# A two-layer hybrid decoder: new tokens in one stationary tile, 1/rms through memory, spatial weights loaded earlier, new tokens' scores behind the attention

## The chip, the cores and the metric

One core of a Trainium2 chip. The metric is the device time of one execution in microseconds (us); smaller is better. The kernel before takes 2384.72 us (median of three runs, 2384.2 to 2386.24).

## The reference

Two layers work on 1024 prompt positions and on 8 new tokens (one for each of 8 requests), which share the weights. All numbers are fp32. Of each layer this matters here:

```python
h = rms_norm(x, norm_g)
(a_b, a_c, a_h, a_gate, s_q, s_k, s_v, s_gate,
 c_u, c_v, c_gate, d_q, d_k, d_v, d_gate) = split(h @ w_in)
...
vn  = layer_norm(c_v, v_ln_g, v_ln_b)
y_c = c_u * (tril(w_spatial) @ vn + b_spatial)
...
for g, (win, dil) in enumerate(((128, 1), (512, 4), (2048, 16))):
    o, lse = attention(dq[g], dk[g], dv[g])
alpha = softmax(lses, axis=0)
y_d = concat(o[g] * alpha[g])
merged = sum(sigmoid(h @ w_merge) * ((branch * silu(gate)) @ w_branch))
x = x + merged @ w_out
```

Branch A is a short convolution, B a sliding-window attention, C the mix over chunks of 128 positions with the matrices w_spatial (six of 128x128), D an attention over three pairs of heads ("groups" 0 to 2) with growing stride, whose three results are weighted by alpha. The new tokens attend to cached keys and values.

## The kernel before

**Products.** x, normalised but for the factor 1/rms, lies with channels on the partitions: eight tiles hh[k] of the rounded (hi) part and eight tiles hl[k] of the rest, 1032 columns each, the first 8 of them the new tokens. Every weight tile is split in the same way (`split_w`: ACT makes wh, POOL makes wl). A product takes three matmuls per 128 channels: hi x hi, lo x hi and hi x lo. Most go through `fm_tile` and `mm_cols` (lines 178 to 182), weights stationary, 344 columns moving. The results go through three accumulators of PSUM ("acc").

**Values.** Where rows must lie on the partitions, `tm_group` (line 341) makes the tokens stationary and moves the weights: eight blocks of 128 tokens and a ninth (n = 8) of the 8 new ones, 24 matmuls each (lines 372, 375, 376). It is called three times in a layer: by `tm_v` for 256 columns (S_V and the first of D_V), then for C_V (384 columns), then by `tm_v` for the other 256 of D_V. In the ninth block the stationary operand has 8 columns.

**1/rms.** The factor 1/rms of a token is multiplied in later. rtok holds it with tokens on the partitions (line 326); rr holds it as a row of 1032 columns, the same on all partitions, and the rotary tables cosT and sinT are multiplied by it. From rtok to rr the kernel makes a diagonal matrix per block (dg, line 332, DVE), multiplies it by ones (line 333, PE), copies the result (line 336, ACT) and multiplies cosT (line 337, DVE) and sinT (line 338, POOL), in three pieces of the row.

**Spatial mix.** Behind the third of these groups lngb (biases and LN factors), and wsp (w_spatial) are loaded; line 465 transposes wsp on PE (six 128x128, "ms" in PSUM).

**New tokens in D and B.** `Decode.scores` (line 647): line 656 transposes the tokens' query, DVE copies it (qr), SP stores it (qscr, line 659) and loads it again on all partitions (qb, line 661); POOL multiplies by the cached keys (line 662), DVE sums up (sd, line 663). `decode_finish` transposes sd (line 680), takes the softmax on DVE and ACT (lines 681 to 709), transposes the weights back (line 713) and gives `values`, six parts of 2 + 16 small matmuls (lines 731 and 733). For the prompt, `attend_d` stores max and denominator of its softmax (sscr, line 872 in group 2); al loads them (line 920), alpha is made on DVE, transposed (line 934), stored (ascr, line 938) and broadcast in six loads (at, line 944). Then y of branch C is loaded from memory (yscr, 516 KB each), split into yh and yl (line 979), and multiplied with w_branch in turn with h @ w_merge.

**Order.** Each engine works its list off in order; a scheduler writes the lists. SP's list holds nearly all loads; `load` (line 90) ties a load to the `dist`-th last mark, a mark being the first matmul of a tile or of every fourth block. A load also waits until its buffer is free and until earlier transfers with the same completion counter have landed. "dec" is a ring of three tiles for v, the cached keys and values, qb, y, lngb, wsp; "ct" one of four.

## Time and profile before

| | |
|---|---|
| median of 3 runs | 2384.72 us |
| profiled execution | 2387.34 us, span 2385.6 us |
| mean granted clock of TensorE | 0.991 |
| PE busy | 2365.5 us (99%) |
| DVE, ACT, POOL busy | 38%, 29%, 35% |
| DMA | 113 GB/s over the span |

The span is what the profile covers, from its first to its last instruction; the time of the execution has a little around it. PE is TensorE, and SP issues transfers. "Granted clock" is the share of 2.4 GHz that the chip let TensorE have. A matmul's time in a timeline reaches beyond the start of the next one, so the cost of one in a stream is the distance of two starts. Rows of the timeline that follow one another and are alike stand in one row with their count (x).

### The profile page before, as it was taken

Reading aid. Unit: us, or ns where it says so; the run is one execution under the profiler, and the core shown is the slowest. Engines: PE = TensorE matmul, PEld = TensorE weight load, DVE = VectorE, ACT = ScalarE, POOL = GpSimd, SP = SyncE. Lnnn points to the kernel's source line nnn. Section 1 sums busy time; section 2 is a strip of 40 time slices with the busy share of each in tenths; the row PEclk is TensorE's granted clock in tenths of the full one; section 3 lists DMA queues with packets and bytes.
Section 4 is the critical chain, followed back from the end, with each engine's and each line's share of the span. In section 5 each row is a group of like instructions: output and inputs, shape, how many; then the busy total and the mean of one; then the engine's idle time right before and its main releaser. Section 6 shows DMA issues by size and latency. Waiting matters only on the chain.

```text
span 2385.6 us, 38754 instructions
## 1 busy us (share of the span) xinstructions
PE 2365.5 (99%) x15896; PEld 2305.1 (97%) x15896; DVE 895.2 (38%) x1938; ACT 687.4 (29%) x1522; POOL 843.5 (35%) x556
## 2 busy tenths in 40 slices
PE   7999999999999999999999999999999999999999
PEld 6999999999999999999999999999999999999999
DVE  4345466335312222324333455554452221213143
ACT  5133432223212222223322244323231221212243
POOL 3333234432223444434442322353322233444330
PEclk9999999999899999999999999999989999999999
DMA  7342423433322212224542423244442122222232
GB/s 237 98 123 79 119 69 109 132 102 106 100 71 88 77 55 97 64 70 123 150 146 72 145 72 98 69 151 113 111 126 67 58 91 66 98 67 62 75 99 101
DMA packets 295962, 235.82 MB, mean 99 GB/s; under 512 B 52756, under 2 KB 279696, under 8 KB 293416
## 3 DMA queue, kind: packets, MB, share of 16 engines
q1 hardware_dynamic: 267952, 206.25, 28.8%
q10 hardware_dynamic: 27832, 27.10, 4.1%
q8 instruction: 124, 2.03, 0.4%
q14 instruction: 54, 0.44, 0.1%
HBM read 192.35 MB, written 76.47 MB: 113 GB/s over the span
## 4 chain that ended last, share of the span: by engine, by line
PE 98%; DVE 1%; DMA 0%; ACT 0%; SPq 0%; issue 0%; ACTq 0%; DVEq 0%
PE acc L181 27%; PE acc L182 27%; PE acc L178 27%; PE acc L372 2%; PE acc L375 2%; PE acc L376 2%; PE sc L540 2%; PE ms L569 2%; PE ms L558 1%; PE ms L733 1%; PE ms L479 0%; PE ms L1042 0%; DMA wr<-in_w_in_dram 0%; DVE xT L264 0%; DVE h0l L209 0%; PE ms L333 0%
## 5 line engine op out<-in xcount | busy, mean ns | idle before, releaser
L156 POOL TENSOR_TENSOR wl<-wr,wh 128x384 fp32r<-128x384 f32 (+2 forms) x228 | 476.9, 2093 | 827.3 <-ACT wh L154 698.7
L181 PE MATMUL acc<-h1l,wh 128*128 128x344 f32 x1584 | 511.5, 323 | 0.0
L182 PE MATMUL acc<-h0h,wl 128*128 128x344 f32 x1584 | 510.4, 323 | 0.0
L178 PE MATMUL acc<-h0h,wh 128*128 128x344 f32 x1584 | 509.3, 322 | 0.9 <-DVE xT L264 0.9
L178 PE MATMUL acc<-h1h,wh 128*128 128x344 f32 x1584 | 510.2, 322 | 0.0
L182 PE MATMUL acc<-h1h,wl 128*128 128x344 f32 x1584 | 509.5, 322 | 0.0
L181 PE MATMUL acc<-h0l,wh 128*128 128x344 f32 x1584 | 508.9, 321 | 0.0
L154 ACT ACTIVATE wh<-wr 128x384 fp32r<-128x384 f32 (+2 forms) x228 | 205.2, 901 | 421.4 <-PE acc L181 393.6
L1005 DVE TENSOR_TENSOR th<-acc,rr 128x344 f32<-128x344 f32 x192 | 99.1, 516 | 553.5 <-PE acc L182 553.5
L181 PEld LDWEIGHTS acc<-h1l,wh 128*128 128x128 f32 x1584 | 299.9, 189 | 4.2 <-issue 3.6
L181 PEld LDWEIGHTS acc<-h0l,wh 128*128 128x128 f32 x1584 | 299.2, 189 | 3.9 <-issue 3.5
L182 PEld LDWEIGHTS acc<-h1h,wl 128*128 128x128 f32 x1584 | 299.7, 189 | 2.8 <-issue 2.3
L178 PEld LDWEIGHTS acc<-h0h,wh 128*128 128x128 f32 x1584 | 299.1, 189 | 2.8 <-issue 1.2
L182 PEld LDWEIGHTS acc<-h0h,wl 128*128 128x128 f32 x1584 | 298.6, 189 | 2.9 <-issue 2.3
L178 PEld LDWEIGHTS acc<-h1h,wh 128*128 128x128 f32 x1584 | 299.6, 189 | 1.4 <-issue 1.0
L1011 POOL TENSOR_TENSOR mg<-mg,th 128x344 f32<-128x344 f32 x144 | 134.0, 931 | 303.3 <-DVE th L1010 303.3
L1006 ACT ACTIVATE th<-th 128x344 f32<-128x344 f32 x192 | 94.3, 491 | 496.9 <-DVE th L1005 496.4
L178 PE MATMUL acc<-yh,wh 128*128 128x344 f32 x576 | 184.4, 321 | 0.0
L182 PE MATMUL acc<-yh,wl 128*128 128x344 f32 x576 | 184.3, 320 | 0.0
L181 PE MATMUL acc<-yl,wh 128*128 128x344 f32 x576 | 184.1, 320 | 0.0
L181 PE MATMUL acc<-ml,wh 128*128 128x344 f32 (+3 forms) x384 | 123.2, 321 | 0.0
L182 PE MATMUL acc<-mh,wl 128*128 128x344 f32 (+3 forms) x384 | 123.0, 321 | 0.0
(278 smaller groups left out, 3256.6 us busy)
## 6 DMA issues: line engine op xcount, KB each, us to landing
wr<-in_w_merge_dram SPq DMA_DIRECT2D x64, 512.0 KB
out_dram<-in_cache_dil_kv_dram SPq DMA_DIRECT2D x128, 255.9 KB
wr<-in_w_in_dram SPq DMA_DIRECT2D x60, 512.0 KB
y<-yscr SPq DMA_DIRECT2D x18, 516.0 KB
wr<-in_w_branch_dram SPq DMA_DIRECT2D x48, 192.0 KB
wr<-in_w_in_dram SPq DMA_DIRECT2D x32, 256.0 KB
wr<-in_w_out_dram SPq DMA_DIRECT2D x16, 512.0 KB
out_dram<-in_cache_dil_kv_dram SPq DMA_DIRECT2D x16, 511.0 KB
```

What stands on the lines that cost most here:

```text
L154: act.activation(hi, raw, AF.Copy)
L156: pool.tensor_tensor(lo, raw, hi.bitcast(F32), op=ALU.subtract)
L178: mm = pe.matmul(ps[:, :n], hi[:, k], xh[k][:, cs], start=(k == 0), stop=False)
L181: pe.matmul(ps[:, :n], hi[:, k], xl[k][:, cs], start=False, stop=False)
L182: pe.matmul(ps[:, :n], lo[:, k], xh[k][:, cs], start=False, stop=(k == kt - 1))
L372: mm = pe.matmul(ps[:M, :N], lh, hi[:, k % kk], start=(k == 0), stop=False)
L375: pe.matmul(ps[:M, :N], ll, hi[:, k % kk], start=False, stop=False)
L376: pe.matmul(ps[:M, :N], lh, lo[:, k % kk], start=False, stop=(k == KT - 1))
L540: pin(pe.matmul(ps[:, h, a * 256:a * 256 + u.nk], u.qs[h], u.ks[h], start=True, stop=True))
L1005: dve.tensor_tensor(t, pg[:, :CH], rr[:, cs], op=ALU.mult)
L1006: act.activation(t, t, AF.Tanh, scale=0.5)
L1011: pool.tensor_tensor(mg[m][:, cs], mg[m][:, cs], t, op=ALU.add)
```

## The change

Four things. (1) The hi and lo columns of the new tokens are copied once per layer into one tile hd of 40 columns (hi in 0 to 7, lo in 32 to 39, zeros between); the ninth block is 16 matmuls in place of 24, and ACT and DVE add the two halves. (2) rtok is stored in a row of memory (rscr, in pieces of 4 bytes) by ACT, and SP loads it on all partitions as rr; cosT and sinT are multiplied once. (3) lngb and wsp are loaded before the second query tile, right behind the call of the first group of values. (4) In D the new tokens' scores are called after the attention of their group.

```diff
--- before.py
+++ after.py
@@ -65,7 +65,7 @@
         return psM.tile([P, 512], F32, tag="ms", name="ms")
 
     def ctmp(name):
-        return tp.tile([P, CH], F32, tag="ct", name=name, bufs=4)
+        return tp.tile([P, MIX], F32, tag="ct", name=name, bufs=4)[:, :CH]
 
     def dscr(name, shape):
         return dr.tile(shape, F32, tag=name, name=name)
@@ -324,18 +324,13 @@
         for ps_, M in ((slice(0, 8), P), (slice(8, 9), NS)):
             act.activation(rtok[:M, ps_], pt_[:M, ps_], AF.Sqrt, bias=epst[:M], scale=1.0 / DM)
             dve.reciprocal(rtok[:M, ps_], rtok[:M, ps_])
-        for n0, n1 in ((8, 9), (0, 4), (4, 8)):
-            ps = pmisc()
-            M = NS if n0 == 8 else P
-            for n in range(n0, n1):
-                dg = sm.tile([P, P], F32, tag="dg", name="dg", bufs=2)
-                dve.tensor_scalar(dg[:M, :M], ident[:M, :M], rtok[:M, n:n + 1], None, op0=ALU.mult)
-                pe.matmul(ps[:, (n - n0) * P:(n - n0) * P + M], onesm[:M], dg[:M, :M], start=True, stop=True)
-            cs = slice(0, NS) if n0 == 8 else slice(NS + n0 * P, NS + n1 * P)
-            w = cs.stop - cs.start
-            act.activation(rr[:, cs], ps[:, :w], AF.Copy)
-            dve.tensor_tensor(cosT[:, cs], cosT[:, cs], rr[:, cs], op=ALU.mult)
-            pool.tensor_tensor(sinT[:, cs], sinT[:, cs], rr[:, cs], op=ALU.mult)
+
+        rscr = dscr(f"rscr{l}", [T])
+        act.dma_start(rscr[0:NS], rtok[:NS, 8])
+        act.dma_start(rscr[NS:T].rearrange("(n i) -> i n", i=P), rtok[:, 0:8])
+        sp.dma_start(rr, rscr.partition_broadcast(P))
+        dve.tensor_tensor(cosT, cosT, rr, op=ALU.mult)
+        pool.tensor_tensor(sinT, sinT, rr, op=ALU.mult)
         cw = sm.tile([P, 3, 3], F32, tag="cw", name="cw")
         for t in range(3):
             load(cw[:, :, t], i["conv_w"][l, t].rearrange("(j p) -> p j", p=P), 2)
@@ -366,6 +361,15 @@
                 cols = blkcols(n) if n < 8 else slice(0, NS)
                 M = P if n < 8 else NS
                 ps = pacc()
+                if n == 8:
+                    for k in range(KT):
+                        for a, w in enumerate(ws[k // kk]):
+                            pe.matmul(ps[:40, :N], hd[:, k], w[:, k % kk], start=(k + a == 0), stop=(k + a == KT))
+                    s = tp.tile([NS, MIX], F32, tag="ct", name="sd", bufs=4)[:, :N]
+                    act.activation(s, ps[32:32 + NS, :N], AF.Copy)
+                    dve.tensor_tensor(s, s, ps[:NS, :N], op=ALU.add)
+                    consumer(n, M, s)
+                    break
                 for k in range(KT):
                     hi, lo = ws[k // kk]
                     lh, ll = hh[k][:, cols], hl[k][:, cols]
@@ -375,6 +379,12 @@
                     pe.matmul(ps[:M, :N], ll, hi[:, k % kk], start=False, stop=False)
                     pe.matmul(ps[:M, :N], lh, lo[:, k % kk], start=False, stop=(k == KT - 1))
                 consumer(n, M, ps[:M, :N])
+
+        hd = sm.tile([P, KT, 40], F32R, tag="hd", name="hd")
+        pool.memset(hd.bitcast(F32), 0.0)
+        for k in range(KT):
+            for a, h in enumerate((hh, hl)):
+                pool.tensor_copy(hd[:, k, 32 * a:32 * a + NS], h[k][:, 0:NS])
 
         vcs = slot("vcs")
         vsam, cvs = vcs[:NS, 0:512], vcs[:NS, 512:512 + MIX]
@@ -406,6 +416,15 @@
 
         kB, qB = rope(kq[0]), [rope(kq[1])]
         tm_v([(S_V, P), (D_V, P)], 0)
+        lngb, wsps = dec([P, T], "lngb"), dec([P, T], "wsp")
+        wsp = wsps[:, 0:6 * P].rearrange("p (g s) -> p g s", g=6)
+        bsps = [lngb[:, 6 * P:7 * P], lngb[:, 7 * P:8 * P], wsps[:, 6 * P:7 * P]]
+        for h in range(2):
+            for j in range(3):
+                load(bsps[j][h * 64:(h + 1) * 64], bview[h, j].partition_broadcast(64), 2)
+        load(lngb[:, 0:MIX], i["v_ln_g"][l].partition_broadcast(P), 2)
+        load(lngb[:, MIX:2 * MIX], i["v_ln_b"][l].partition_broadcast(P), 2)
+        load(wsp, i["w_spatial"][l].rearrange("g t s -> t g s"), 2)
         qB.append(rope_tile(w_pair(l, S_Q, 1), "qB1"))
         cvt = [sl.tile([P, 2, MIX], F32, tag="slot", name=f"cv{q}") for q in range(4)]
         lnst = sm.tile([P, 9, 6], F32, tag="lnst", name="lnst")
@@ -438,14 +457,6 @@
             return t
 
 
-        lngb, wsps = dec([P, T], "lngb"), dec([P, T], "wsp")
-        wsp = wsps[:, 0:6 * P].rearrange("p (g s) -> p g s", g=6)
-        bsps = [lngb[:, 6 * P:7 * P], lngb[:, 7 * P:8 * P], wsps[:, 6 * P:7 * P]]
-        for h in range(2):
-            for j in range(3):
-                load(bsps[j][h * 64:(h + 1) * 64], bview[h, j].partition_broadcast(64), 2)
-        load(lngb[:, 0:MIX], i["v_ln_g"][l].partition_broadcast(P), 2)
-        load(lngb[:, MIX:2 * MIX], i["v_ln_b"][l].partition_broadcast(P), 2)
         for n in range(9):
             M = P if n < 8 else NS
             if n == 0:
@@ -457,7 +468,6 @@
             dve.tensor_tensor(v, v, lngb[:M, 0:MIX], op=ALU.mult)
             dve.tensor_tensor(v, v, lngb[:M, MIX:2 * MIX], op=ALU.add)
         store_later(2, o["chunk_v_s"][l].rearrange("b s c -> (b s) c"), cvs)
-        load(wsp, i["w_spatial"][l].rearrange("g t s -> t g s"), 2)
         wsT = dec([P, 6, P], "wsT")
         for g0 in (0, 3):
             ps = pmisc()
@@ -887,8 +897,8 @@
         decD = Decode("D")
         rows, attention = branch_d(0, ends)
         conv_a(0, rows)
+        attention()
         decD.scores(0, dqs[0], dks[0])
-        attention()
         conv_a(1)
         in_a(0)
         decB = Decode("B")
@@ -903,15 +913,15 @@
         rows, attention = branch_d(1)
         in_a(1)
         rows()
+        attention()
         decD.scores(1, dqs[1], dks[1])
-        attention()
         out_a(1)
         conv_a(2)
         rows, attention = branch_d(2)
         sg0 = gate_d(0)
         rows()
+        attention()
         decD.scores(2, dqs[2], dks[2])
-        attention()
         in_a(2)
         values_d = decD.finish(OD)
 
```

The scheduler orders the lists anew. In the rows here line numbers of the changed kernel are up to 10 higher.

**PE, first group of values, layer 0** (acc and ms are PSUM tiles, h0h and h0l the parts of h, dg the diagonal matrix). Before:

```order
229 L372 MATMUL acc<-wh,h0h_132 128x256
230 L375 MATMUL acc<-wh,h0l_140 128x256
231 L333 MATMUL ms<-dg,onesm 128x8
232 L333 MATMUL ms<-dg,onesm 128x128
233 L376 MATMUL acc<-wl,h0h_132 128x256
```

Changed; the group begins at row 217:

```order
287 L379 MATMUL acc<-wh,h0l_143 128x256
288 L380 MATMUL acc<-wl,h0h_135 128x256
289 L475 MATMUL ms<-ident,wsp 128x128 x6
290 L376 MATMUL acc<-wh,h0h_128 128x256
291 L379 MATMUL acc<-wh,h0l_136 128x256
```

Line 333 is gone from the group, and the six transposes of wsp, which stood behind the third group, come after 72 of its matmuls. It is so in both layers.

**SP, at the same place, layer 0.** Before (the loads of lngb and wsp stood in rows 37 to 43, behind the second weights of the third group):

```order
26 L93 DMA cosT<-const_cos_dram 128x1032
27 L93 DMA sinT<-const_sin_dram 128x1032
28 L93 DMA wr<-in_w_in_dram 128x2x384 x3
29 L93 DMA out_dram<-in_cache_swa_kv_dram 4x2x16256
30 L93 DMA wr<-in_w_in_dram 128x2x384
```

Changed:

```order
28 L93 DMA wr<-in_w_in_dram 128x2x384
29 L93 DMA lngb<-in_b_spatial_dram 64x128 x2
30 L93 DMA wsp<-in_b_spatial_dram 64x128
31 L93 DMA lngb<-in_b_spatial_dram 64x128
32 L331 DMA rr<-rscr_526 128x1032
33 L93 DMA lngb<-in_b_spatial_dram 64x128
34 L93 DMA wsp<-in_b_spatial_dram 64x128
35 L93 DMA lngb<-in_v_ln_g_dram 128x384
36 L93 DMA lngb<-in_v_ln_b_dram 128x384
37 L93 DMA wsp<-in_w_spatial_dram 128x6x128
38 L93 DMA wr<-in_w_in_dram 128x2x384 x2
```

rr's load and all of lngb and wsp stand ahead of three of the four weight loads of C_V; rr waits for the two stores of rscr, and the load of v_ln_b (row 36) for the counter that rr's landing raises. In layer 1 rr stands right ahead of v_ln_b, which doesn't wait for it.

**PE, branch D of layer 0, end of group 2's attention** (line 569, 579 in the changed kernel). Before:

```order
3237 L182 MATMUL acc<-h0h_132,wl 128x344
3238 L569 MATMUL ms<-pt,v_5477 64x128 x4
3239 L680 MATMUL ms<-ident,sd 8x128 x6
3240 L178 MATMUL acc<-h0h_133,wh 128x344
3241 L181 MATMUL acc<-h0l_141,wh 128x344
```

Changed, at the same place:

```order
3199 L579 MATMUL ms<-pt,v_5432 64x128 x4
3200 L666 MATMUL ms<-ident,dqs_5304 8x128
3201 L690 MATMUL ms<-ident,sd 8x128 x2
3202 L181 MATMUL acc<-h0l_139,wh 128x344
3203 L182 MATMUL acc<-h0h_131,wl 128x344
```

Changed, at the first matmul with yh (pn and pd are the transposed weights, vcs and cD the new and cached values):

```order
3326 L743 MATMUL ms<-pd,cD_5727 64x1 x8
3327 L741 MATMUL ms<-pn,vcs 64x8
3328 L743 MATMUL ms<-pd,cD_5727 64x1 x8
3329 L178 MATMUL acc<-yh_6133,wh 128x344
3330 L178 MATMUL acc<-h0h_128,wh 128x344
```

Line 656, ahead of the attention before, is now behind it (row 3200), and the transposes of sd come in three pairs: 21 wide matmuls lie between the first and the second, 50 between the second and the third, and 39 between the third and line 723 (713 before). Before, 73 lay between line 680 and line 713, 20 more ahead of the values and 12 between them and the first matmul with yh; now the six parts follow line 723 in one piece and the first matmul with yh follows at once.

## Rows read from the trace of the kernel before

**Rows 1.** The page: span, and busy time of each engine (share, instructions).
```profile
span 2385.6 us, 38754 instructions
...
PE 2365.5 (99%) x15896; PEld 2305.1 (97%) x15896; DVE 895.2 (38%) x1938; ACT 687.4 (29%) x1522; POOL 843.5 (35%) x556
```

**Rows 2.** Waits of PE, whole span: in total, times, longest (us).
```profile
PE ms L333 <- DVE dg L332: 3.8, 3, 1.5
```

**Rows 3.** PE timeline, layer 0: start us, us, engine line op operands xcount [idle before].
```profile
50.42 0.28 PE L372 MATMUL acc<-wh,h0h 128*128 128x256 f32 x1
...
51.60 0.28 PE L375 MATMUL acc<-wh,h0l 128*128 128x256 f32 x1
...
79.92 0.28 PE L372 MATMUL acc<-wh,h0h 128*8 128x256 f32 x1
...
82.67 0.32 PE L178 MATMUL acc<-h0h,wh 128*128 128x344 f32 x1
...
127.55 0.34 PE L372 MATMUL acc<-wh,h0h 128*8 128x384 f32 x1
...
131.80 0.38 PE L540 MATMUL sc<-kB,qB 64*128 64x128 f32 x2
```

**Rows 4.** PE timeline, layer 1: first group of values, first and next matmul.
```profile
1222.38 0.38 PE L372 MATMUL acc<-wh,h1h 128*128 128x256 f32 x1
...
1251.61 0.32 PE L178 MATMUL acc<-h1h,wh 128*128 128x344 f32 x1
```

**Rows 5.** Stretches: PE, PEld, DVE, ACT, POOL busy (count), PEclk, DMA share, GB/s.
```profile
56.80:60.20 3.40, 3.40 (x19) 3.40 (x18) 0.29 (x1) 0.00 (x0) 0.00 (x0) 0.50 0.97 241
599.50:613.20 13.70, 13.70 (x91) 13.57 (x90) 7.00 (x9) 3.38 (x4) 2.52 (x2) 0.50 0.95 245
1770.30:1784.00 13.70, 13.70 (x91) 13.54 (x92) 6.85 (x9) 3.11 (x4) 3.80 (x2) 0.50 0.95 247
```

**Rows 6.** DVE timeline: end of 1/rms, both layers.
```profile
51.51 0.15 DVE L326 RECIPROCAL rtok<-rtok 8x1 f32<-8x1 f32 x1 [1.27 <-ACT rtok L325]
...
1222.79 0.29 DVE L326 RECIPROCAL rtok<-rtok 128x8 f32<-128x8 f32 x2 [21.97 <-ACT rtok L325]
```

**Rows 7.** ACT queue, SP queue, DVE: sscr in 16-byte pieces, then al.
```profile
571.81 0.63 ACTq L872 DMA_DIRECT2D sscr<-std  x1
...
577.31 0.37 SPq L920 DMA_DIRECT2D al<-sscr  x1
...
580.43 0.17 DVE L924 TENSOR_TENSOR mx<-al 128x16 f32<-128x16 f32 x1 [2.38 <-DMA al<-sscr]
```

**Rows 8.** SP queue, POOL, DVE: the new tokens' query rows in branch D.
```profile
342.62 0.30 SPq L659 DMA_DIRECT2D qscrD<-qr  x1
...
343.90 0.35 SPq L661 DMA_DIRECT2D qb<-qscrD  x1
...
347.92 2.40 POOL L662 TENSOR_TENSOR qb<-qb,cD 128x1024 f32<-128x1024 f32 x1 [0.84 <-DMA qb<-qscrD]
...
350.35 1.22 DVE L663 TENSOR_REDUCE sd<-qb 128x16 f32<-128x1024 f32 x1 [0.48 <-POOL qb L662]
```

**Rows 9.** SP queue: the six broadcasts of the prompt's group weights.
```profile
595.17 4.04 SPq L944 DMA_DIRECT2D at<-ascr  x6
```

**Rows 10.** DVE and ACT: softmax of the new tokens, then the first yh.
```profile
582.47 1.01 DVE L681 TENSOR_SCALAR sx<-ms 8x384 f32<-8x384 f32 x2
...
589.27 0.95 DVE L709 TENSOR_TENSOR sx<-sx,dw 8x774 f32<-8x774 f32 x1
...
606.91 1.06 ACT L979 ACTIVATE yh<-y 128x1032 fp32r<-128x1032 f32 x1 [10.53 <-DMA y<-yscr]
```

**Rows 11.** PE timeline, layer 0: end of D's attention, transposed weights, first yh.
```profile
579.79 0.66 PE L569 MATMUL ms<-pt,v 128*64 128x128 f32 x8
...
592.64 0.53 PE L713 MATMUL ms<-ident,sx 8*128 8x8 f32 x6
...
610.92 0.49 PE L178 MATMUL acc<-yh,wh 128*128 128x344 f32 x1
```

## The prediction

> **What bounds the kernel now.** I read the page's busy line first. TensorE (PE) is busy for 2365.5 us of a span of 2385.6, while VectorE (DVE), ScalarE (ACT) and GpSimd (POOL) stay under 40% [rows 1]. So an instruction taken from another engine gains nothing by itself, and time comes from three things only: fewer PE instructions, PE waits, and PE's clock. The list of PE's waits comes next: away from the start of the program its only large entry is the 1/rms matmul of line 333, 3.8 us in three waits [rows 2]. Then I read PE's timeline where the change touches it, and the granted clock by stretch. The clock falls to half (1.2 of 2.4 GHz) at 56.8 us for 3.4 us, and at the end of branch D of each layer for 13.7 us [rows 5]. The profiled execution took 2387.34 us, 2.6 above the median of 2384.72; the terms below come from its trace and are added to the median. About 0.2% (4.8 us) is what a measurement can tell from no change.
>
> **New tokens in one stationary tile.** In the group of 256 columns the prompt's matmuls start ten apart in 51.60-50.42 us, so one costs 0.118 us. The 24 with 8 stationary columns run from 79.92 to 82.67, so one costs 0.115; with 384 columns they run from 127.55 to 131.80, 0.177 each [rows 3]. The change makes 16 out of 24: eight less, in two groups at 0.115 and one at 0.177, in two layers: 2 x 8 x (0.115+0.115+0.177) = **6.5 us less**. The new ones have 40 stationary columns. That 8 and 128 columns cost the same to 0.003 us [rows 3] is why I charge nothing for the width.
> The Trainium skill, "TensorE: Matmul & The Clock Gate", section "LDWEIGHTS (loading the stationary operand)", says that the load grows with the number of columns, columns/1.2 ns. By that an estimate is 27 ns more for 40 columns than for 8, and if the load set the pace the 96 new matmuls would give back 2.6 of the 6.5 us; the rows at 8 and at 128 columns contradict that, so the sum leaves it out.
> The 16 copies per layer that fill the tile lie on POOL and are wanted only by the ninth block of a group; POOL is 35% busy [rows 1]. If that cover went, PE would wait there for a copy or two. The addition of the two halves per group, and the cosine and sine multiplied once instead of in three pieces, lie on ACT, DVE and POOL with the same cover; all of this I cost at nothing.
>
> **1/rms through memory.** Line 333 and what it did to the first group of values go. In layer 0 the group lasts from 50.42 to 82.67, 32.25 us [rows 3]. Its own matmuls are worth 192 x 0.118 + 24 x 0.115 = 25.4, so 6.8 us were lost to line 333, its waits and the half clock at 56.8. In layer 1 it lasts from 1222.38 to 1251.61 [rows 4], 29.2, so 3.8 were lost. Together **10.6 us less**, if nothing takes their place.
>
> **Spatial weights one group ahead.** Something does. PE now meets the six transposes of the spatial weights after only 72 matmuls of that group, 72 x 0.118 = 8.5 us after its start: 58.9 us in layer 0, 1230.9 in layer 1. Those weights stand on SP's queue behind the broadcast of 1/rms (rr), which has to wait for the store of 1/rms, and in layer 0 the load before them (v_ln_b) waits in turn for rr's landing.
> Layer 0: 1/rms is there at 51.66 [rows 6]. The store has 4-byte pieces. Bounds: 5.5 us, from the issue of sscr (1024 pieces of 16 bytes) at 571.81 to al's, which waits for it, at 577.31 [rows 7]; and 1.3 us, qscr's eight rows of 512 bytes, 342.62 to 343.90 [rows 8]. I take 5.5, since its pieces are nearest in size. rr is a broadcast of 516 KB; its neighbour qb (512 KB) takes 4.0 us, 343.90 to 347.92 [rows 8]. That makes 51.7+5.5+4.0 = 61.2, and with two issues of 0.37 [rows 7] 61.9. The spatial weights (393 KB) need between al's 3.1 us [rows 7] and qb's 4.0: they land at 65.0 to 65.9, and PE waits for 6 to 7 us. With the short store it would be 2 to 3. I take 6.0, and 1.7 for a stretch at half clock behind it, like that of 3.4 us at 56.8 [rows 5]: 7.7.
> ACT, whose stores and rotary copies share completion counters, is late too and so the evictions of these blocks are, but three accumulators hold exactly those 72 matmuls, so PE meets that delay at the same place and under the same wait.
> Layer 1: 1/rms at 1223.1 [rows 6], store 5.5, three issues of 0.37: the weights start at about 1229.5 beside rr, and land 3.1 us later if undisturbed, 8 if they share with all of rr: 1232.6 to 1237.5, a wait of 1.7 to 6.6; none with the short store. I take 3.5, and 0.9 for the clock: 4.4. Together **12.1 us more** (bounds 2 and 19).
>
> **Scores behind the attention.** For the first group of D and for the second the new tokens' chain has hundreds of matmuls before its result is read, and I cost it at nothing. For the third it is read at once. Between the last attention matmuls of D and the first with yh there are 105 wide matmuls now and 110 then, so the attention ends 0.8 us earlier, at 579.0 instead of 579.8 [rows 11]. The query's transpose now comes behind it, and on DVE its copy behind the prompt's softmax, which waits for al and ends at about 582. From there: store to broadcast 1.3, broadcast 4.0, POOL 2.4, DVE 1.2 [rows 8]: the scores are there at about 591.5, up to 592.7 with a slower broadcast. PE gets there after 71 matmuls of 344 columns, each 344/256 x 0.118 = 0.158, and 1 us of transposes, at about 591.3. The softmax then takes 582.47 to 590.22, 7.75 us [rows 10], while only 39 matmuls (6.2 us) are left beside it, so the transposes of the weights (line 713) run at about 600.0 instead of 592.64 [rows 11]. What hangs on them keeps its distance: behind line 713 stand the transposed group weights, their store, six broadcasts of 4.0 us of issue [rows 9], and only then y's first load on SP. Before, yh began 606.91-592.64 = 14.3 us after line 713 and took 1.06 [rows 10, 11]. So the first matmul with yh can run at 600.0+15.3 = 615.3, against 610.92 before [rows 11]: 4.4 us more. Before, 20 and 12 matmuls and the values filled that stretch; now the values alone do, and then PE stands. Half clock lasted 2.3 us beyond 610.92 [rows 5], a loss of 1.1; I expect 1 us more of it. So 5.4 per layer; layer 1 has the same half-clock stretch [rows 5], and I take the same. **10.8 us more** (bounds 3 and 16).
>
> **Sum:** -6.5-10.6+12.1+10.8 = +5.8, so **2390.5 us**.
>
> **The rivals.** (1) *The D end costs nothing.* Place: the first matmul with yh. If y lands within 10 us of line 713 instead of 14.3, because the values no longer hold its buffers, PE finds it there and the 10.8 fall away: 2384.72-6.5-10.6+12.1 = 2379.7, faster. For it: the buffers of the cached values come free sooner, since the six parts run in one piece. Against it: y's first load was issued as soon as the six broadcasts were (595.17+4.04) [rows 9], so the buffer didn't hold it. It decides from a landing at 610 on.
> (2) *The store is quick.* At qscr's 1.3 us [rows 8] the wait for the spatial weights shrinks to 2 us in layer 0 and nothing in layer 1: 2384.72-17.1+2+10.8 = 2380.4.
> (3) *The store is slow.* If 4-byte pieces take twice what 16-byte pieces took, 11 us, each layer waits 5.5 us longer: 2401.5. For it: 1024 pieces of 16 bytes took 5.5 us and eight of 512 bytes 1.3 [rows 7, 8], so pieces and not bytes set the price. Against it: the count of pieces is the same as sscr's.
> The Trainium skill, "DMA: Bandwidth & Descriptors", section "Specifications", says that a transfer under 512 bytes is read, changed and written back, which speaks against this part of the change; the two stores of the trace agree, and whether 4 bytes are dearer than 16 no row shows.
>
> **How the numbers follow.** Forecast 0.50, its own range 2384 to 2397: two thirds of it lie above 2389.5. Rival 1: 0.20, 2374 to 2385, 0.12 of it faster. Rival 2: 0.13, half of it faster. Rival 3: 0.12, slower. Rivals 1 and 2 together (about 2370): 0.05, faster. Faster is 0.12+0.06+0.05 = 0.23; slower 0.33+0.12 = 0.45; the same 0.32. The range takes the lower ends of rivals 1 and 2 and the high bounds of the forecast, 2384.72-17.1+17+16 = 2400.6, and leaves out the joint case and most of rival 3: 2376 to 2400.5.
>
> **What would show it.** In the profile after: six fewer busy us in the groups' last blocks; no line 333; PE's list of waits with the spatial transposes (line 475 there), longest about 6 us at 59 us, waiting for w_spatial; a second wait, of 5 us or so, at the first matmul with yh in each layer; a small one at line 723; and half clock behind each. It is wrong if line 475 waits for less than 3 us, if the first matmul with yh comes less than 12 us behind line 723, or if blocks with 40 columns start 0.14 us apart or more.

## The result and the profile after

The changed kernel takes 2419.12 us (median of four, 2417.68 to 2419.52), the kernel before 2384.46 on the same chip (2381.6 to 2386.24): 1.0145 times as long, 95% interval 1.0128 to 1.0163, or about 34.7 us more. The direction was predicted, the size was not: 2390.5 was forecast and 2400.5 was the upper end. The profiled execution took 2419.22 us, its span is 2417.5, and the mean granted clock 0.985 instead of 0.991. The two spans differ by 31.9 us and not by 34.7, since the profiled execution of the kernel before (2387.34) was 2.9 above its median here.

The page of the changed kernel, to set beside [rows 1]:

```profile
span 2417.5 us, 38609 instructions
...
PE 2362.2 (98%) x15812; PEld 2304.4 (95%) x15812; DVE 890.3 (37%) x1922; ACT 692.6 (29%) x1526; POOL 862.2 (36%) x586
```

PE is busy for 3.3 us less in a span that is 31.9 us longer, so the whole loss is waiting, and matmuls at half clock. The list of PE's waits of the changed kernel (in total, times, longest, us), of the entries that the change made:

```profile
PE ms L475 <- DMA wsp<-in_w_spatial_dram: 21.4, 2, 10.8
PE ms L723 <- DVE sx L719: 9.3, 2, 5.0
PE acc L178 <- ACT yh L989: 5.0, 2, 3.1
```

The mechanism of each was foretold: line 475 waits for w_spatial, line 723 and the first yh wait at the end of D, and line 333 is gone [rows 2]. But line 475 waits 10.8 and 10.6 us where about 6 and 3.5 were expected, line 723 waits 5.0 where "a small one" was, and the first yh waits 1.9 and 3.1 where 5 were. Starts on PE in the two traces show where the time is lost:

| PE starts (us) | before | after | later by |
|---|---|---|---|
| first group of values, layer 0 | 50.42 | 52.83 | 2.4 |
| behind that group | 82.67 | 91.28 | 8.6 |
| scores of B, behind C_V | 131.80 | 139.06 | 7.3 |
| first matmul with yh, layer 0 | 610.92 | 626.26 | 15.3 |
| first group of values, layer 1 | 1222.38 | 1238.92 | 16.5 |
| behind that group | 1251.61 | 1276.68 | 25.1 |
| first matmul with yh, layer 1 | 1782.17 | 1813.20 | 31.0 |
| end of the span | 2385.6 | 2417.5 | 31.9 |

The first groups lose 6.2 and 8.5 us, where +12.1 and -10.6 together had made +1.5 of both; between B's scores and layer 1 some 9 us go, and about 7 in layer 1.

The granted clock by stretch of the changed kernel answers to [rows 5] (columns as there):

```profile
29.40:32.80 3.40, 3.40 (x14) 3.40 (x13) 3.40 (x4) 2.90 (x7) 2.91 (x3) 0.50 0.87 335
63.50:77.20 13.70, 4.84 (x23) 4.87 (x24) 10.74 (x7) 1.21 (x3) 8.24 (x4) 0.50 0.96 240
609.70:630.10 20.40, 17.58 (x128) 17.04 (x129) 8.07 (x13) 3.21 (x4) 2.49 (x1) 0.50 0.69 170
1251.40:1261.60 10.20, 3.31 (x14) 2.94 (x15) 3.49 (x4) 1.21 (x3) 4.64 (x2) 0.50 0.96 273
1797.50:1818.00 20.50, 17.43 (x126) 17.13 (x126) 9.18 (x11) 3.19 (x3) 3.45 (x2) 0.50 0.69 169
```

In the two stretches of the first groups (63.5 and 1251.4) PE is busy for only 4.84 and 3.31 us, the rest is the wait itself; half clock thus cost about half of these, 2.4 and 1.7 us. At the end of D PE works 17.5 us at half clock instead of 13.7 [rows 5], 1.9 us more in each layer.

The chain of the first group in layer 0, from the timeline of all engines in the changed kernel (ACTq and SPq are the queues in which ACT and SP issue DMAs; to evict an accumulator is to copy its result out of PSUM, here line 401, so that it can be used again):

```profile
51.49 0.39 ACTq L330 DMA_DIRECT2D rscr<-rtok  x1
52.91 0.53 ACTq L329 DMA_DIRECT2D rscr<-rtok  x1
53.67 0.61 ACTq L290 DMA_DIRECT2D qs<-kB  x1
60.38 1.90 ACTq L290 DMA_DIRECT2D qs<-kB  x3
60.50 0.34 SPq L331 DMA_DIRECT2D rr<-rscr  x1
62.37 5.55 ACTq L290 DMA_DIRECT2D qs<-qB  x4
...
65.22 2.36 POOL L333 TENSOR_TENSOR sinT<-sinT,rr 128x1032 f32<-128x1032 f32 x1 [8.78 <-DMA rr<-rscr]
65.25 3.42 DVE L332 TENSOR_TENSOR cosT<-cosT,rr 128x1032 f32<-128x1032 f32 x1 [12.37 <-DMA rr<-rscr]
66.03 0.38 SPq L93 DMA_DIRECT2D wsp<-in_w_spatial_dram  x1
67.97 1.21 ACT L401 ACTIVATE vn<-acc,rtok 128x256 f32<-128x256 f32 x3 [13.21 <-DMA qs<-qB]
72.36 1.51 PE L475 MATMUL ms<-ident,wsp 128*128 128x128 f32 x6 [10.83 <-DMA wsp<-in_w_spatial_dram]
```

SP's side is the predicted chain with longer links: the store runs from 51.49 to about 60.4 (8.9 us, 5.5 were charged), rr takes 4.7, w_spatial 6.3 (66.03 to 72.36; 3.1 to 4.0 were charged) in a stretch where the DMA engines are 96% busy (the window from 63.5). But ACT's side is late too: its second load of a rotary copy (qs) issues at 60.38, when the store lands (it waits for the completion counter that the store raises), the eighth is issued at 67.9, and only then does ACT evict the first three blocks (67.97). In layer 1 the two sides end together; there the store was issued at 1240.10, and the second load of qs at 1247.66. The third row below holds the seventh and eighth load, which are part of the row above it:

```profile
1241.11 8.36 ACTq L290 DMA_DIRECT2D qs<-kB  x4
1249.56 9.67 ACTq L290 DMA_DIRECT2D qs<-qB  x4
...
1258.07 1.16 ACTq L290 DMA_DIRECT2D qs<-qB  x2
...
1259.28 1.21 ACT L401 ACTIVATE vn<-acc,rtok 128x256 f32<-128x256 f32 x3 [19.31 <-PE ms L475]
```

The transposes began at 1258.18 there, the evictions at 1259.28. The row names line 475 as what released the evictions, but ACT's queue was issuing qs until 1259.23. That the two end together is no accident: the seventh load waits for a completion counter which in this trace w_spatial's load raises, so it is issued when w_spatial lands, and in layer 1 ACT's lateness hangs on SP's.

### The profile page after: what moved, and what is told of

Read it like the earlier page. It is cut to its first block, busy times and chain, and to the rows that moved or that the text cites. A ratio compares the mean times of both kernels' runs of the same rounds, so it can differ in the third digit from the quotient of the medians.

```text
span 2417.5 us, 38609 instructions
## 1 busy us (share of the span) xinstructions
PE 2362.2 (98%) x15812; PEld 2304.4 (95%) x15812; DVE 890.3 (37%) x1922; ACT 692.6 (29%) x1526; POOL 862.2 (36%) x586
## 4 chain that ended last, share of the span: by engine, by line
PE 91%; DMA 4%; DVE 2%; ACT 1%; SPq 1%; issue 1%; POOL 0%; ACTq 0%; POOLq 0%; DVEq 0%
PE acc L178 26%; PE acc L182 26%; PE acc L181 26%; PE acc L376 2%; PE acc L380 2%; PE acc L379 2%; PE sc L550 2%; PE ms L579 2%; PE ms L568 1%; DMA wr<-in_w_in_dram 1%; DMA rscr<-rtok 1%; DMA y<-yscr 1%; DMA wsp<-in_w_spatial_dram 1%; DVE h0l L209 1%; PE ms L489 0%
## 5 line engine op out<-in xcount | busy, mean ns | idle before, releaser
L156 POOL TENSOR_TENSOR wl<-wr,wh 128x384 fp32r<-128x384 f32 (+2 forms) x228 | 486.1, 2134 | 800.4 <-ACT wh L154 747.2
```

Of the source, the lines that this page charges most:

```text
L156: pool.tensor_tensor(lo, raw, hi.bitcast(F32), op=ALU.subtract)
```

## Experiments

The expectations speak of two theories of the first group: A, SP's chain to w_spatial alone costs it; B, ACT's queue does, by the qs loads behind the store of 1/rms. D1 and D2 are two of the end of D: D1, the query's row is made too late; D2, the softmax is longer than the matmuls beside it. "The mark" is the first matmul of the ninth block, which the kernel before reports to `load` and the changed one doesn't. Ratios are to the kernel before on the same chip. The runs lie on several chips, on which the kernel before had medians from 2384.5 to 2386.7, so a difference of 2 us between runs of different chips says nothing.

### One part undone

**e1: lngb and w_spatial loaded where they were before.**

```diff
         tm_v([(S_V, P), (D_V, P)], 0)
-        lngb, wsps = dec([P, T], "lngb"), dec([P, T], "wsp")
...
-        load(wsp, i["w_spatial"][l].rearrange("g t s -> t g s"), 2)
         qB.append(rope_tile(w_pair(l, S_Q, 1), "qB1"))
```

> The changed kernel with part 3 undone: lngb and wsp are loaded where they were before, behind the third group of values. Theory A (the loss in the first group of values of each layer is PE waiting for w_spatial at line 475, 10.8 and 10.6 us, and the half clock behind each, 13.7 and 10.2 us long): both go, no wait of PE over 1 us stays in the group, the group falls to about 26 us in each layer, and the time to 2419 - 21.4 - 12 = about 2386 to 2394. Theory B (the 4-byte store of 1/rms holds up ACT's queue, whose loads of qs share its completion counters, so the evictions of the first blocks come late, and line 475 is only the place where PE stood when it happened): PE waits at the fourth block instead, for ACT's eviction, 4 to 6 us in each layer with half clock behind it, and the time is 2400 to 2412.

2420.82 us, 1.0147 (1.0132 to 1.0162): nothing gained, and slower than either theory said. PE's waits:

```profile
PE acc L376 <- ACT vn L401: 15.4, 2, 8.0
PE ms L723 <- DVE sx L719: 9.1, 2, 5.0
PE ms L475 <- DMA wsp<-in_w_spatial_dram: 5.4, 2, 3.3
```

With w_spatial out of the way PE stands at the next block for want of an evicted accumulator, for 15.4 us instead of 21.4, and waits 5.4 us more for w_spatial in the third group (the lost mark, see e7): 20.8 us in all. ACT's first eviction in that group comes at 67.57, behind the last qs issue. A alone falls, and B's wait is there, with 7.4 and 8.0 us instead of 4 to 6. ACT's queue is late by itself, and one wait had hidden the other.

**e2: 1/rms by matmul again** (lines 327 to 333 of the changed kernel replaced by lines 327 to 338 of the kernel before).

```diff
-        act.dma_start(rscr[0:NS], rtok[:NS, 8])
-        act.dma_start(rscr[NS:T].rearrange("(n i) -> i n", i=P), rtok[:, 0:8])
-        sp.dma_start(rr, rscr.partition_broadcast(P))
...
+                pe.matmul(ps[:, (n - n0) * P:(n - n0) * P + M], onesm[:M], dg[:M, :M], start=True, stop=True)
```

> The changed kernel with part 2 undone: rr is again made by nine diagonal matrices and matmuls, nothing of 1/rms goes through memory. The transposes of w_spatial still stand after 72 matmuls of the first group. Theory A: w_spatial no longer stands behind rr's load on SP and starts some 10 us earlier, so the wait at line 475 falls under 3 us and the half clock behind it to 3 to 7 us; the matmuls and waits of the diagonal matrices come back (10.6 us in both layers by the prediction). Time 2419 - 21 + 3 - 8 + 10 = about 2403. Theory B: the same direction, as ACT's queue is free: about 2400 to 2405. If w_spatial is late for another reason (its place on SP behind other loads), the wait stays near 10 us and the time near 2425.

2402.24 us, 1.0069 (1.0054 to 1.0084): 16.9 us less than the change. The transposes still come after 72 matmuls, and no wait for w_spatial is left; evictions wait 2.0 us, line 333 3.0. So the place of the transposes costs nothing by itself: the store behind 1/rms made both waits.

**e3: all scores ahead of the attention again, and e8: only those of group 2.**

```diff
         rows()
+        decD.scores(2, dqs[2], dks[2])
         attention()
-        decD.scores(2, dqs[2], dks[2])
```

> The changed kernel with part 4 undone: in D the new tokens' scores are called ahead of the attention, as before. Theory A (the D end costs 10 us in layer 0 and 9 in layer 1: line 723 waits 5.0 and 4.4 us for the softmax, the first matmul with yh 1.9 and 3.1, and half clock lasts 20.5 instead of 13.7 us): the waits at line 723 go, the half clock at the D end is 13.7 us again, and the time is 2419 - 19 = about 2400. Rival (the D end is long because everything behind the first group is shifted against the loads, not because of the order of scores): less than 5 us gained.

> The changed kernel with the scores of D's third group alone called ahead of the attention; groups 0 and 1 behind it as in the change. Theory C (the D end's 16 us of e3 come from the third group only, whose scores are read at once): about 2403, as e3. Rival (the calls for groups 0 and 1 cost too, by what they shift on SP and in the dec ring): 2407 to 2415.

2402.92 us, 1.0078 (1.0061 to 1.0095), and 2403.1, 1.0073 (1.0055 to 1.0091). Both are 16 us below the change, so the third group alone makes the loss, and moving the other two is free, as the prediction costed it.

**e4: the ninth block as 24 matmuls again, with its mark.**

```diff
-        hd = sm.tile([P, KT, 40], F32R, tag="hd", name="hd")
...
-                if n == 8:
-                    for k in range(KT):
...
-                    break
```

> The changed kernel with part 1 undone: the ninth block is again 24 matmuls of 8 columns, with its mark. The scheduler then puts the transposes of w_spatial after the second group (432 matmuls later than the first group's start) instead of after 72 matmuls. Theory A: the waits at line 475 and their half clock go (33 us of wait and clock), 6.5 us of matmuls come back: about 2393 to 2400, although only the part that saves matmuls is undone. Theory B: PE waits at the fourth block for ACT's evictions instead, 4 to 6 us per layer and half clock behind: 2408 to 2418.

2430.27 us, 1.0184 (1.0168 to 1.0201): 11.2 slower than the change, more than the 6.5 us of its matmuls, and slower than either theory said. Evictions wait 13.6 us (`PE acc L367 <- ACT vn L386`), and no transposes stand in the first group: the mark moves them behind the second. A second run without w_spatial's wait that still loses the group, as e1. In layer 1 PE also waits 4.6 us for a rotary tile of D (dqp), where it waits at most 1.1 in the other runs; why, and where the rest goes, stays open.

### The store, ACT's queue and the mark

**e5: the same 1/rms transposed on PE and stored in rows of 512 bytes.**

```diff
-        act.dma_start(rscr[NS:T].rearrange("(n i) -> i n", i=P), rtok[:, 0:8])
+        pe.transpose(ps[:8, 0:P], rtok[:, 0:8], ident)
...
+        dve.tensor_copy(rrow[:, 0:P], ps[:8, 0:P])
...
+        act.dma_start(rscr[NS:T].rearrange("(n i) -> n i", i=P), rrow[:, 0:P])
```

> The changed kernel, with rtok transposed on PE first (two small transposes, DVE copies) and stored as eight rows of 512 bytes and one of 32 instead of 1024 pieces of 4 bytes; order otherwise the same, transposes of w_spatial after 72 matmuls. Theory B1 (the store of 4-byte pieces, 8.9 and 7.5 us from issue to landing, sets both waits, as rr, the loads behind rr on SP and the loads of qs on ACT wait for it): the store takes 1.3 to 2 us, 0.7 us are added for the copies, all that follows comes 6 us earlier, the waits at line 475 fall from 10.8 and 10.6 to about 5 us each, with less half clock: 2419 - 12 - 4 = about 2403. Theory B2 (the chain is long because rr, qs, lngb and wsp all load at once; the store only shifts them): waits at line 475 of 8 us or more stay, time above 2410.

2402.85 us, 1.0072 (1.0055 to 1.0089): the time as expected, the waits not, so the match is partly luck. In layer 0 SP issues rr 3.0 us behind the last issue of the store (53.82, 56.83) instead of 7.6 (52.91, 60.50), in layer 1 1.1 us instead of 7.5. The wait for w_spatial, of which some 5 us per layer were to stay, is gone; evictions wait 7.4 us in both layers together instead, and layer 0's first group takes 32.9 us. So the store's pieces made the wait for w_spatial, and with a quick store ACT's queue remains.

**e11: the change with the mark back.**

```diff
-                            pe.matmul(ps[:40, :N], hd[:, k], w[:, k % kk], start=(k + a == 0), stop=(k + a == KT))
+                            mm = pe.matmul(ps[:40, :N], hd[:, k], w[:, k % kk], start=(k + a == 0), stop=(k + a == KT))
+                            if k + a == 0:
+                                mark(mm)
```

> The changed kernel with a mark in the ninth block, all four parts kept. The transposes of w_spatial move from after 72 to after 416 matmuls. As in e1 and e4, ACT's queue, held by the loads of qs behind the 4-byte store, is then what PE meets: a wait for the evictions of 6 to 8 us in each first group, and 2416 to 2424. If the place of the transposes were the cause, 2390 to 2400.

2412.8 us, 1.0106 (1.0091 to 1.0122). The transposes are behind 416 matmuls now and wait for nothing, the evictions wait 15.0 us. That is nearer to B's number than to the one by which the place of the transposes was all; the 6.3 us gained are those by which 15.0 is less than 21.4.

**e12: e11 with the qs loads of the first two rotary tiles on POOL's queue.**

```diff
-                act.dma_start(qs[a * 32:(a + 1) * 32, :], q[b * 32:(b + 1) * 32, :])
+                (pool if first else act).dma_start(qs[a * 32:(a + 1) * 32, :], q[b * 32:(b + 1) * 32, :])
...
-        kB, qB = rope(kq[0]), [rope(kq[1])]
+        kB, qB = rope(kq[0], first=True), [rope(kq[1], first=True)]
```

> e11 (the change with a mark in the ninth block), with the eight loads of qs for the first two rotary tiles issued on POOL's queue instead of ACT's. Store, rr and everything else as in e11. Theory B, queue part (the evictions are late because ACT issues the loads of qs in order, and the second of them waits for the store's completion counter): the waits for evictions in the first groups, 15.0 us in three, fall under 4 us and the half clock of 6.8 us behind each goes or halves: 2412.8 - 11 - 5 = about 2397. If the evictions are late because they themselves need something that the store delays, the waits stay and the time is above 2408.

2398.19 us, 1.0056 (1.0041 to 1.0072): 14.6 less than e11 by the medians and 12 by the ratios, by this alone. ACT's first eviction comes at 54.43, the moment its block ends, though the store and rr are no quicker (rr issued at 60.67). PE's timeline, first group of layer 0, and the two windows over the first groups (columns as in rows 5):

```profile
51.19 0.28 PE L378 MATMUL acc<-wh,h0h 128*128 128x256 f32 x1
...
75.76 0.32 PE L178 MATMUL acc<-h0h,wh 128*128 128x344 f32 x1
```

```profile
51.00:77.00 26.00, 26.00 (x219) 25.96 (x218) 11.43 (x6) 6.34 (x14) 18.34 (x13) 1.00 0.71 178
1222.00:1250.00 28.00, 28.00 (x236) 27.93 (x235) 9.00 (x6) 6.67 (x13) 16.03 (x13) 1.00 0.72 172
```

The group takes 24.6 us in layer 0 (32.2 before, 38.4 in the change) and 24.7 in layer 1, with PE busy throughout at full clock. This is the run that settles the first group. One wait of the kind is left: at the start of C_V in layer 1 PE waits 3.7 us for ACT to evict a query tile (qB), and ACT's queue has just held two stores for 5.3 us:

```profile
1259.53 5.33 ACTq L417 DMA_DIRECT2D out_dram<-vcs  x2
```

**e7: part 1 alone in the kernel before; e9: the same with the mark; e10: e9 and w_spatial early.** (Diffs as in the change and in e11.)

> The kernel before with part 1 alone. The prediction's term: 6.5 us less, 2378. If the wider stationary tile cost time (27 ns each by columns), 2380.5. If the mark that the ninth block no longer makes shifts loads so that something comes late, 2384 or more.

> Part 1 alone as in e7, but the ninth block's first matmul makes a mark again, so loads tied to the last marks are issued where they were before; the transposes of w_spatial come right behind the third group, in one piece. Theory M (e7 lost its 6.5 us because the missing mark lets loads and with them the transposes move forward, into the third group, where PE waited 3.1 and 1.8 us for w_spatial, with half clock behind them): no wait for w_spatial over 0.5 us, no half clock in the stretch of branch B's attention, time 2378 to 2381. Rival (the 40-column tile itself, or its copies on POOL at the start, cost what the fewer matmuls gave): as e7, 2388 to 2394.

> e9 with part 3 added: spatial weights loaded one group ahead, 1/rms by matmuls, scores first. The transposes come after 416 matmuls of the groups, in the second group's last block. Theory M: w_spatial is there long before, no wait, time as e9, 2378 to 2381. Rival (part 3 alone delays the weight loads of C_V behind lngb and wsp on SP): PE waits in the second group, 2384 or more.

e7: 2392.16 us, 1.0033 (1.0021 to 1.0046), slower than before although it has fewer matmuls. e9: 2383.89, 0.9984 (0.9973 to 0.9995). e10: 2383.45, 0.9987 (0.9976 to 0.9999). In e7 PE waits, as nowhere in e9:

```profile
PE ms L480 <- DMA wsp<-in_w_spatial_dram: 4.9, 2, 3.1
```

The lost mark, one of those by which loads are tied, let loads and with them the transposes move forward into the third group; that costs 8.3 us by the two medians and 12 by the two ratios (the profiled execution of e7 is one of its fastest, 2387.92, so the row shows less). e7 came out as the third of its cases, and for that reason. The rival, that the tile or its copies eat up all that the matmuls give, falls with e9. e10 shows that loading w_spatial early is free where nothing ahead of it on SP waits. But e9 and e10 miss 2378 to 2381: e9 gains 2 to 4 us (medians, ratio) of the 6.5 that its matmuls are worth. What takes the rest, the copies and additions of part 1 or something else, stays open.

**e6: parts 1 and 2 with the row store, without the mark.** (Part 3 undone as in e1, part 4 as in e3, the store as in e5.)

> Parts 1 and 2 alone, part 2 with the row store: spatial weights late, scores ahead of the attention. Theory B1: the evictions' wait (15.4 us in two in e1) falls to 4 us or less in both layers; first groups near 28 us each; time 2384.5 - 6.5 - 10.6 + 4 + 3 = about 2375. Theory B2: the loads of qs still hold ACT until 12 us after the group's start; waits of 5 us per layer stay, time 2383 to 2390.

2392.97 us, 1.0031 (1.0018 to 1.0043). A miss: evictions still wait 8.1 us (ACT's queue) and the transposes 6.2 for w_spatial, as in e7 (the lost mark). The profiled execution was the slowest of ten, 2399.03.

### The end of branch D

**e13: the copy of the query's rows on ACT** (e11 with one line).

```diff
-                dve.tensor_copy(qr, ps[:NS, :P])
+                act.activation(qr, ps[:NS, :P], AF.Copy)
```

> e11 with the copy of the new tokens' query (qr) on ACT instead of DVE. Theory D1 (in the change qr stands behind the prompt's softmax on DVE, which waits for al; that delay of some 3 us is what line 725 then waits for): qr comes 2.5 to 3 us earlier in D's third group, the waits for the scores and the softmax fall from 9.7 us in both layers to 4, time about 2405 to 2408. Theory D2 (the softmax itself is slowed: 9.6 us from its first to its last DVE operation instead of 7.75, one operation of 3.2 us instead of 0.95 while POOL splits a weight tile): the collision may move but the waits stay above 7 us, time 2409 to 2414.

2412.85 us, 1.0109 (1.0096 to 1.0123), no different from e11 and inconclusive: on ACT the copy stands behind the exponential of alpha (ew), which waits for al like DVE's work, and behind more work that waits for DVE. It ran at 586.36, where the other engine's had run only 0.4 us later.

**e15: on DVE the first operation on al is tied behind that copy** (on top of e11).

```diff
-                dve.tensor_copy(qr, ps[:NS, :P])
+                self.copied = dve.tensor_copy(qr, ps[:NS, :P])
...
-        dve.tensor_tensor(mx, al[:, :, 0, 0:2], al[:, :, 1, 0:2], op=ALU.max)
+        with tc.issue_after(decD.copied.ins):
+            dve.tensor_tensor(mx, al[:, :, 0, 0:2], al[:, :, 1, 0:2], op=ALU.max)
```

> e11 with the prompt's first DVE operation on al tied behind the copy of the new tokens' query row (qr) of D's third group; PE's order is unchanged. Theory D1 (qr stands behind al on DVE): qr comes 3.5 us earlier, at once after its transpose; the scores are there without a wait, and the wait at line 725 falls from 5.0 and 4.0 us to 1.5 and 1; 2412.8 - 7 = 2404 to 2407, or less if half clock shortens. Theory D2 (the softmax beside POOL is what is long): waits at line 725 stay above 3.5 us, 2409 or more.

2407.89 us, 1.0087 (1.007 to 1.0103): 4.9 below e11. PE's wait at the transposed weights (line 725 here), layer 0 and layer 1, from its timeline:

```profile
603.59 0.54 PE L725 MATMUL ms<-ident,sx 8*128 8x8 f32 x6 [3.35 <-DVE sx L721]
...
1784.92 0.54 PE L725 MATMUL ms<-ident,sx 8*128 8x8 f32 x6 [4.09 <-DVE sx L721]
```

In layer 0 the copy runs at 582.09, ahead of al, and the stretch from the first transposes of sd to the values shrinks from 26.2 us in e11 to 22.4: D1. In layer 1 the scores are there 1.6 us before they are wanted, and PE still waits 4.1; there it is the softmax. DVE, and POOL beside it:

```profile
1775.54 1.01 DVE L693 TENSOR_SCALAR sx<-ms 8x384 f32<-8x384 f32 x2 [0.33 <-PE ms L692]
...
1779.26 2.33 DVE L713 TENSOR_TENSOR dmm<-dmm,dm 8x2 f32<-8x2 f32 x1
...
1783.91 0.95 DVE L721 TENSOR_TENSOR sx<-sx,dw 8x774 f32<-8x774 f32 x1
```

```profile
1778.11 3.46 POOL L156 TENSOR_TENSOR wl<-wr,wh 128x1024 fp32r<-128x1024 f32 x1 [5.96 <-DMA out_dram<-in_cache_dil_kv_dram]
```

From 1775.54 to 1784.86 it takes 9.3 us, with about 5.2 us of wide matmuls beside it, and an operation on 8x2 elements, 0.14 us elsewhere, takes 2.33 while POOL splits a weight tile. D2 holds there; neither theory alone does, and the time lies between the two.

### A version that beats both

**e14: parts 1 and 2, mended** (part 1 with the mark of e11, the row store of e5, qs on POOL of e12; parts 3 and 4 left out). **e16: the same with the 4-byte store.**

> Parts 1 and 2 with what the runs so far point to: row store of 1/rms, loads of qs for the first two tiles on POOL, mark in the ninth block; spatial weights late and scores first. Theory: no wait of PE over 1.5 us in the first groups, which fall to 25 to 27 us (before: 32.2 and 29.0), no line 333; 8 to 10 us less than before, 2375 to 2378, and 6 below e9. Rival (rr through memory makes the rotary tables late, and with them something further on, the attention of B or the loads of C_V): 2380 or more.

> e14 with the 4-byte store of 1/rms again. If the queue is the whole cause (evictions behind the loads of qs), 2372 to 2375 as e14, though rr comes 6 us later. If the store's length matters by itself, through rr, the rotary tables and what waits for them: 2377 or more.

e14: **2372.67 us** (2371.8 to 2373.29), 0.9942 (0.993 to 0.9955), about 13.6 us faster than the kernel before. e16: 2374.77, 0.9943 (0.9929 to 0.9958). The 13.6 us of e14 are less than the 17.1 which the prediction had worked out for these two parts, and more than the 8 to 10 that were expected of e14. PE's waits for ACT in e14:

```profile
PE acc L384 <- ACT qB L281: 0.8, 1, 0.8
...
PE acc L384 <- ACT vn L409: 0.7, 1, 0.7
```

Neither lies in a first group: from 40 to 90 us and from 1200 to 1260 PE waits for nothing, and the groups take 24.9 and 25.0 us. With qs off ACT's queue the slow store matters by 2 us at most (e16, within its expectation). So where the transposes of w_spatial stand behind the first group, the store's length was the size of the delay and ACT's order what let it reach PE; in the change itself SP's order let it through as well.

## Why the prediction was wrong in size

**The matmuls saved (-6.5): right on the spot, not confirmed as a whole.** Blocks with 40 columns run at the pace that was charged. Matmuls in the last block of the first group of the changed kernel:

```profile
90.33 0.28 PE L367 MATMUL acc<-wh,hd 128*40 128x256 f32 x1
...
91.15 0.28 PE L367 MATMUL acc<-wl,hd 128*40 128x256 f32 x1
```

Seven starts apart in 0.82 us, 0.117 each; and over the stretch with C_V the lag in the table falls by 1.3 us, where 8 x 0.177 were charged. That the width costs nothing held too. As a whole the term is not confirmed: e9 gains 2 to 4 us. What it left out is the mark, which the prediction didn't see: the diff drops `mark(mm)` with the old branch and says nothing of it.

**1/rms through memory (-10.6): right, but hidden.** In e12 the first group takes 24.57 us in layer 0 and 24.7 in layer 1; 25.4 less 0.9 for the eight matmuls saved were worked out. The gain was there as soon as nothing took its place.

**Spatial weights (+12.1): the step that failed.** It measured 21.4 us of waits and 4.1 of clock, 25.5; over the 24.6 us of e12 the two groups (38.45 and 37.76) are 27.0 too long. Two things were wrong. First the sizes: the store was taken at 5.5 us because "its pieces are nearest in size" and took 8.9 in layer 0 and 7.6 in layer 1, between the forecast and the 11 us of rival 3. w_spatial was taken at 3.1 to 4.0 and took 6.3 and 9.2 (1248.98 to 1258.18), while rr, the qs loads and other transfers filled the DMA engines (96% in both windows); no run takes these away alone. The Trainium skill, "DMA: Bandwidth & Descriptors", section "Specifications", warns of transfers under 512 bytes. The runs agree: e5 took 4.6 us off the store's landing in layer 0 and 6.4 in layer 1. But e5 also makes 9 pieces out of 1032, and whether their size or their number did it no run here shows. Second the cause: the text had seen that ACT "is late too" and dismissed it, since PE would meet both delays "at the same place and under the same wait". That is true, and it is why taking away one of them (e1, e4, e11) gained little or nothing. But ACT's delay was never worked out, and so charged as if it were no longer than the other. e1, where ACT's side is left alone, prices it at 7.4 us in layer 0 and 8.0 in layer 1. By that, PE would have waited longer than the 6.0 and 3.5 us that were charged even with w_spatial as early as forecast. A delay under the same wait doesn't cost nothing: the longer of the two is the term, and both have to be worked out.

**Scores behind the attention (+10.8): the mechanism right, the size too small.** Undoing it gave back 16.2 us (e3), 16.0 by the third group alone (e8). By the table the stretches in which it lies lost 10.2 us in layer 0 (15.3-7.3, 0.9 for the ninth block of D_V that is saved on the way, 1.2 up to the first group of layer 1) and 9.2 in layer 1 (31.9-25.1, and 2.3 for two ninth blocks). So some 3 of these 19.4 us aren't this part's, and what they are stays open. The timeline of the changed kernel, layer 0:

```profile
581.75 0.37 SPq L930 DMA_DIRECT2D al<-sscr  x1
...
586.73 0.18 DVE L934 TENSOR_TENSOR mx<-al 128x16 f32<-128x16 f32 x1 [7.79 <-DMA al<-sscr]
...
589.04 0.27 DVE L668 COPY qr<-ms 8x128 f32<-8x128 f32 x1
...
590.56 0.33 SPq L671 DMA_DIRECT2D qb<-qscrD  x1
...
595.43 2.40 POOL L672 TENSOR_TENSOR qb<-qb,cD 128x1024 f32<-128x1024 f32 x1 [3.67 <-DMA qb<-qscrD]
...
597.87 1.22 DVE L673 TENSOR_REDUCE sd<-qb 128x16 f32<-128x1024 f32 x1 [4.31 <-POOL qb L672]
...
600.99 1.01 DVE L691 TENSOR_SCALAR sx<-ms 8x384 f32<-8x384 f32 x2
602.96 2.39 POOL L156 TENSOR_TENSOR wl<-wr,wh 128x1024 fp32r<-128x1024 f32 x1 [5.12 <-ACT wh L154]
603.01 3.16 DVE L700 TENSOR_TENSOR sx<-sx,dm 8x774 f32<-8x774 f32 x1
...
609.61 0.95 DVE L719 TENSOR_TENSOR sx<-sx,dw 8x774 f32<-8x774 f32 x1
610.62 0.81 PE L723 MATMUL ms<-ident,sx 8*128 8x8 f32 x6 [4.95 <-DVE sx L719]
...
617.69 7.03 SPq L93 DMA_DIRECT2D y<-yscr  x3
626.26 0.65 PE L178 MATMUL acc<-yh,wh 128*128 128x344 f32 x1 [1.90 <-ACT yh L989]
```

Each link is the predicted one. The copy qr stands behind the prompt's softmax, which waits for al; the first yh runs 626.26-610.62 = 15.6 us behind line 723, and 15.3 was said. al took 5.0 us instead of 3.1 [rows 7], qb 4.9 instead of 4.0, the softmax began 1.9 us behind the scores, with two operations of another branch ahead of it on DVE, and took 9.6 us instead of 7.75. Line 700 alone is 2.2 us longer: 3.16 us, where the same operation had taken 0.95 in the kernel before (DVE timeline there):

```profile
584.80 0.95 DVE L690 TENSOR_TENSOR sx<-sx,dm 8x774 f32<-8x774 f32 x1
```

The softmax now falls into a stretch in which POOL splits a weight tile. So line 723, for which "a small" wait was written, waits 5.0 and 4.4 us, and half clock, charged 1 us more, cost 1.9. Rival 1 is refuted (y came no sooner), rival 2 as well (the store was not quick).

**The range.** Its upper end was added up with 17 us for the spatial weights, although their own bound was 19. With 19 it would have been 2402.6, and the result lies far outside that too.

**The start (+2.4)** wasn't in the prediction and isn't tied to the change: the stretch at half clock from 29.4 us, of 3.4 us, comes in e9, which has no other part than the first, and not in e12, which has all four and starts its first group at 51.19, nor in e13, which differs only in D from e11, where it comes. At half clock 3.4 us cost 1.7; the other 0.7, and what brings the stretch on, stay open.

## What to carry to other kernels

Where two waits fall on the same instruction, work out both to their ends: the list of waits names only the later one, and undoing one part shows nothing until the other is gone too. On an engine that issues DMAs and also evicts accumulators, a load that must wait for an earlier transfer holds the evictions behind it, so before a slow store is put on that queue, look what stands next there and which completion counter it waits for. And a branch that replaces another also drops the bookkeeping in it: compare the order of the loads, not the arithmetic alone.

## What the runs showed of the hardware

A store of 1024 pieces of 4 bytes took 8.9 and 7.6 us, where as many pieces of 16 bytes had taken 5.5 [rows 7]; fewer bytes in as many pieces were no cheaper. Other transfers were hardly in the way: the DMA engines were 12 and 14% busy meanwhile (51.5 to 60.4 and 1240.1 to 1247.7 us), and 60% beside the 16-byte store (571.8 to 577.3 us in the kernel before). The same numbers in nine pieces (e5) landed 3.0 and 1.1 us behind the last issue, against 7.6 and 7.5.

DVE stood for as long as an operation of POOL lasted. Line 332 and line 333 start together, at 65.25 and 65.22; POOL's takes 2.36 us and DVE's 3.42; in layer 1 it is the other way, 3.41 and 1.23. Line 700 ended 0.82 us behind POOL's line 156. The Trainium skill, "SBUF — State Buffer", section "SBUF: two separate sides", calls the port pair of the two an exclusive lock, taken for a whole instruction. These rows agree: the later of the two ends behind the other by about its own time (DVE 1.09 of 1.23 and 0.82 of 0.95 us, POOL 2.21 of 2.36).

A weight load grows with its columns and still doesn't set the pace of matmuls with 256 moving columns. In the traces loads of 8, 40 and 128 columns take 0.09, 0.11 and 0.19 us, while the matmuls start 0.115 to 0.118 us apart with each of them ([rows 3] and line 367 above):

```profile
79.92 0.09 PEld L375 LDWEIGHTS acc<-wh,h0l 128*8 128x8 f32 x1
...
60.33 0.19 PEld L375 LDWEIGHTS acc<-wh,h0l 128*128 128x128 f32 x1
```

These are of the kernel before; in the changed one the loads of line 367 (40 columns) have a median of 0.114 us.
